# Order of the seven products where a stage ends, and of the last plain part, in a two-layer decoder trunk

## The chip, the cores and the metric

The kernel runs on one core of a Trainium2 chip (trn2). The metric is the device time of one execution in microseconds (us). The engines named below are PE (TensorE, matmuls), DVE (VectorE), ACT (ScalarE), POOL (GpSimd) and SP (SyncE, which here mostly issues loads).

## The reference

The input is 512 tokens of width 1024 in float32. Two layers follow one another, and a last norm closes:

```python
for l in range(DEPTH):                       # DEPTH = 2
    x = x + 0.5 * swiglu(rms_norm(x, ffn1_norm[l]), ffn1_wg[l], ffn1_wu[l], ffn1_wd[l])
    h = rms_norm(x, mix_norm[l])
    z = h @ w_in[l]                          # q, k, v and three conv inputs
    ...                                      # sliding-window attention, short convolution
    x = x + concat([attn_out, conv_out]) @ w_out[l]
    x = x + 0.5 * swiglu(rms_norm(x, ffn2_norm[l]), ffn2_wg[l], ffn2_wu[l], ffn2_wd[l])
return rms_norm(x, final_norm)

def swiglu(h, w_gate, w_up, w_down):         # 1024 -> 2816 -> 1024
    return (silu(h @ w_gate) * (h @ w_up)) @ w_down
```

## The kernel before

**Arithmetic.** Every large product is made of three matmuls: weight and activation are each split in a high and a low part (`wh`, `wl`; `xh`, `xl`), and high x high, high x low and low x high are added in PSUM. The weight split is one copy on ACT and one subtraction on DVE (`split`, L195 and L196). `split_far` (L198) makes the low part in another way: ACT writes the negative, ACT copies, and POOL issues a DMA that adds the raw data.

**Sevens.** Most of the weights are multiplied by a scheme of seven products instead of eight (Strassen-Winograd). Weight quarters and their sums are named a11, a12, s2, s3, s1, a22, s4; the activation quarters and sums that go with them b11, b21, t2, t3, t1, t4, b22. Within b11, b21, b12, b22 the second digit is the half of the tokens (half 0 is tokens 0 to 255). A product of a `share` seven (down projection, or `w_out` in the mixing stage) is two groups of 12 matmuls of 512 columns, 24 matmuls in all. `share` (L751) runs seven steps in the order `CHAINS2`. Each step names an accumulator and an operand. Accumulators x (tag "mm"), y ("sc") and w ("aux") are two PSUM banks each; a step whose flag is False goes on in the banks that hold earlier products. After each step two `scalar_tensor_tensor` on DVE (L771) add the banks to a part of the residual stream `x`: `SHARES` says which column half o, which token half t, and the sign.

```python
CHAINS = (
    ("x", "b11", True), ("w", "b21", True), ("x", "t2", False), ("y", "t3", True),
    ("x", "t1", False), ("y", "t4", False), ("x", "b22", False),
)
CHAINS2 = CHAINS[:4] + (CHAINS[5], CHAINS[4], CHAINS[6])
```

So in a `share` seven y t4 follows y t3, and x t1 is followed by x b22. `Seven.make` prepares the operands: sums on DVE (L540 to L545), then a split on ACT and DVE, or `split_far` for the names in `far` (in the mixing stage t1, t4 and b22).

**Weights.** `order` is the list of weight groups, made by `plan`, and `take_split` takes them one by one. It prepares splits `SPLIT_AHEAD` = 2 groups ahead (`need_split`); `wh` and `wl` have three buffers each. Raw tiles are loaded `LOAD_AHEAD` = 4 units ahead. Sums of weights are made in `need_split`: s2 on DVE (L222, which adds s1 to a11 in place, in the raw tile that a far split's DMA also reads), s4 with an accumulating DMA that POOL issues (`share`) or on DVE (L247). In each feed-forward part that begins with a seven, the first weight group (b = 0, a11, h = 0) is marked "far" and split by `split_far`.

**Stages.** A feed-forward part is a list of stages: "w" sevens for gate and up, "u" a last such block, "p" plain blocks, "s" the down projection of four blocks as a `share` seven, "d" the down projection of single blocks as plain products (`down`, L283, matmuls at L294, additions to x at L1006: for each column half o, for each block, for each of the four token tiles t, 6 matmuls). `FIRST` is the first part of layer 0 and ends with ("s", 6). `INNER` and `LAST` end with ("d", (8, 9, 10)). A mixing stage ends with its `share` seven for `w_out`. In all there are seven `share` sevens that do not end a stage list, and three that do; two of the plain parts of three blocks hand over to a further norm.

**Norm at a stage end.** Where a stage ends, `Norm` is called with `after(t, o)` behind the last addition to each of the eight parts of x. `__call__` squares the part on ACT (L472). When the four parts of a token half are there, `stage` takes the root (an ACT function of another table, so there is a table load before L491), refines it on DVE (L492, L383 to L385), writes xn (L507, DVE), transposes it on PE (L512), and copies the transposes: to a high and low part for a mixing stage (L515 ACT, L516 DVE), or to `hf` for a feed-forward part (L518, ACT), where b11, b21 and t2 are then made at once. `ENDS` says after which step of `share` which part of x is complete. In the last of these norms, `Finale` takes over.

**Order on the engines.** A scheduler orders the instructions of each engine from the program text and the dependences; what the text makes later can be pulled ahead where its operands are there. `tc.issue_after` holds an instruction behind another.

Of the kernel before, what the change touches and what calls it, by code (L numbers as in the profile page):

```python
# [15 lines left out]
P = 128  # L16
D = 1024
S = 512
# [23 lines left out]
SHARED = ("a11", "a12", "s2", "s3", "a22", "s1", "s4")  # L42

SHARES = ((0, 0, 1), (0, 0, 1), (1, 0, -1), (1, 1, 1), (1, 0, 1), (1, 1, -1), (0, 1, 1))
ENDS = {1: (0, 0), 4: (1, 0), 5: (1, 1), 6: (0, 1)}
# [14 lines left out]
CHAINS2 = CHAINS[:4] + (CHAINS[5], CHAINS[4], CHAINS[6])  # L60
# [3 lines left out]
def trunk_kernel(  # L64
# [139 lines left out]
    def need_split(g):  # L204
        while state["split"] <= min(g, len(order) - 1):
# [37 lines left out]
            if isinstance(order[n][1], tuple):  # L243
                if what == "s3" and how == "share":
                    nc.gpsimd.dma_start(out=a12, in_=a11, accum_op=ALU.add)
                elif what == "s3":
                    nc.vector.tensor_add(a12, a12, a11)  # L247
                done = {"s3": (0, 3), "s1": (1,), "a22": (4,), "s4": (2,)}.get(what, ())
                for i in done:
                    del raw_of[u + 2 * i + h]  # L250
# [32 lines left out]
    def down(acts, blocks):  # L283

        for o in range(2):
            accs = [psum("mm", [P, S], f"down_{state['group']}_{t}") for t in range(NT)]
            for i, b in enumerate(blocks):
                _, wh, wl = take_split()
                ah, al = acts[b]
                for t in range(NT):  # L290
                    tok = slice(t * P, (t + 1) * P)
                    for k in range(2):
                        for n, (a, w) in enumerate(((ah, wh), (al, wh), (ah, wl))):
                            nc.tensor.matmul(  # L294
                                accs[t],
                                a[:, k, tok],
                                w[:, k, :],
                                start=i + k + n == 0,
                                stop=i + 1 == len(blocks) and k == 1 and n == 2,
                            )  # L300
                    if i + 1 == len(blocks):
                        yield t, o, accs[t]

    def plan():
# [14 lines left out]

        def seven(at, how, forms=SHARED):  # L320

# [5 lines left out]
            order.extend((u, (what, h, how(what, h))) for what in forms for h in range(2))  # L327

        def ffn(wg, wu, wd, stages):
            for what, b in stages:  # L330
# [4 lines left out]
                if what == "w":  # L335
                    seven(
                        lambda o, j, h: ((wg, wu)[o], KC // 2 * j + 2 * h, 2, 2 * b * P, S),
                        lambda what, h: "far" if (b, what, h) == (0, "a11", 0) else None,
                        FORMS,
# [1042 lines left out]
```

## Time and profile before

| what | value |
|---|---|
| time, median of 3 runs | 1748.76 us |
| lowest, highest | 1743.51, 1749.88 us |
| profiled execution, own time | 1748.8 us |
| its span | 1747.0 us |
| mean granted clock of TensorE | 0.988 |
| busy: PE, DVE, ACT, POOL | 1691.9, 1334.4, 966.9, 194.6 us |
| matmuls | 8150 |

The span is the time from the first to the last recorded instruction of the profiled execution; its own time also holds what lies around it. Places in the profile are given in us from the span's start. The stage ends of interest lie at about 346 (first seven of that kind, into mixing), 517 (mixing into a feed-forward part), 868 (plain part into a feed-forward part), 1219 (plain part into mixing) and 1393 (mixing into a feed-forward part). In rows of single instructions the columns are: start, duration, engine, line, operation, output <- input, shapes, count of neighbours put together, and in brackets the engine's idle time before it with what ended it.

### The profile page before, as it was taken

To read this page: it belongs to the slowest core of one execution; us is meant where nothing else is said; L and a number is where in the kernel's file an instruction comes from. 1 tells how busy PE (TensorE), PEld (TensorE's weight loads), DVE (VectorE), ACT (ScalarE), POOL (GpSimd) and SP (SyncE) were. 2 spreads that over 40 slices of the span, in tenths; PEclk is the share of its full clock that TensorE was granted. 3 is DMA by queue.
4 is the path that set the end of the run, shared out by engine and by line. 5 is a ranking of instruction groups with operands and counts; after the bars stand their busy time and mean duration, and the time that the engine had idled before them with its cause. 6 is when DMAs were issued, how large, how long until landed. Compare 5 with 4: busy or idle time off the path is not lost. (4 is left out here: it accounts for less than half of the span.)

```text
span 1747.0 us, 21808 instructions
## 1 busy us (share of the span) xinstructions
PE 1691.9 (97%) x8150; PEld 1408.2 (81%) x8150; DVE 1334.4 (76%) x1741; ACT 966.9 (55%) x1379; POOL 194.6 (11%) x175
## 2 busy tenths in 40 slices
PE   9999999999989999999999999999999899999998
PEld 7888897798868888877778888877988678888777
DVE  7986689858778776798487776984587797767983
ACT  6545565556666555654365555543465665556553
POOL 0011111000210111110101111100002201111101
PEclk9999999999998999999989999999999999999999
DMA  8467787622695776777637776784126957777771
GB/s 241 108 181 190 184 204 204 158 61 62 163 234 143 186 178 180 192 186 201 145 114 200 182 180 183 193 203 120 37 61 154 242 146 187 176 180 193 189 185 49
DMA packets 188638, 287.19 MB, mean 164 GB/s; under 512 B 9172, under 2 KB 72180, under 8 KB 188532
## 3 DMA queue, kind: packets, MB, share of 16 engines
q1 hardware_dynamic: 146340, 204.91, 36.8%
q0 software_dynamic: 41488, 80.23, 27.2%
q8 instruction: 64, 1.05, 0.2%
q10 hardware_dynamic: 704, 0.66, 0.1%
q14 instruction: 42, 0.34, 0.1%
HBM read 268.46 MB, written 2.10 MB: 155 GB/s over the span
## 5 line engine op out<-in xcount | busy, mean ns | idle before, releaser
L195 ACT CAST wh<-raw 128x1024 fp32r<-128x1024 f32 (+1 forms) x500 | 520.8, 1045 | 572.4 <-PE x L742 134.2
L196 DVE TENSOR_TENSOR wl<-raw,wh 128x1024 fp32r<-128x1024 f32 (+1 forms) x500 | 604.5, 1213 | 291.8 <-ACT wh L195 290.3
L742 PE MATMUL x<-wh,fb 128*128 128x512 f32 x608 | 188.7, 391 | 0.0
L742 PE MATMUL x<-wh,ft 128*128 128x512 f32 x608 | 188.6, 391 | 0.0
L742 PE MATMUL y<-wh,ft 128*128 128x512 f32 x608 | 188.2, 391 | 0.0
L742 PEld LDWEIGHTS x<-wh,fb 128*128 128x128 f32 x608 | 114.4, 188 | 23.5
L742 PEld LDWEIGHTS x<-wh,ft 128*128 128x128 f32 x608 | 113.1, 188 | 22.8
L742 PEld LDWEIGHTS y<-wh,ft 128*128 128x128 f32 x608 | 113.1, 188 | 22.7
L742 PE MATMUL x<-wl,fb 128*128 128x512 f32 x304 | 118.5, 390 | 0.0
L742 PE MATMUL x<-wl,ft 128*128 128x512 f32 x304 | 118.3, 389 | 0.0
L742 PE MATMUL y<-wl,ft 128*128 128x512 f32 x304 | 118.0, 389 | 0.0
L190 POOL DMA_DIRECT2D raw<-in_ffn_wu_dram x42 | 51.1, 1217 | 596.2 <-DVE wl L196 295.2
L742 PE MATMUL w<-wh,fb 128*128 128x512 f32 x304 | 100.6, 415 | 13.3 <-ACT wh L195 10.8
L274 PE MATMUL acc<-hh,wh 128*128 128x512 f32 x240 | 94.6, 394 | 0.0
L277 PE MATMUL acc<-hh,wl 128*128 128x512 f32 x240 | 94.0, 391 | 0.0
L275 PE MATMUL acc<-hl,wh 128*128 128x512 f32 x240 | 93.6, 390 | 0.0
L294 PE MATMUL down<-wh,a 128*128 128x512 f32 x288 | 89.0, 390 | 0.0
L742 PE MATMUL x_s<-wh,ft_s 128*128 128x512 f32 x256 | 79.5, 398 | 8.3 <-ACT wh L195 8.0
L742 PE MATMUL y_s<-wh,ft_s 128*128 128x512 f32 x256 | 80.8, 395 | 3.9 <-ACT wh L195 2.7
L742 PE MATMUL x_s<-wh,fb_s 128*128 128x512 f32 x256 | 80.1, 393 | 3.9 <-DVE x L771 3.6
L222 DVE TENSOR_TENSOR raw<-raw,raw 128x1024 f32<-128x1024 f32 x58 | 70.2, 1219 | 15.7 <-DMA wl<-raw 15.2
L742 PEld LDWEIGHTS w<-wh,fb 128*128 128x128 f32 x304 | 58.5, 198 | 28.0 <-ACT wh L195 13.1
(304 smaller groups left out, 3429.5 us busy)
## 6 DMA issues: line engine op xcount, KB each, us to landing
raw<-in_ffn_wu_dram SPq DMA_DIRECT2D x129, 512.0 KB, 3.7
raw<-in_ffn_wd_dram SPq DMA_DIRECT2D x104, 512.0 KB, 5.1
raw<-in_ffn_wg_dram SPq DMA_DIRECT2D x86, 512.0 KB, 4.8
raw<-in_ffn_wu_dram POOLq DMA_DIRECT2D x42, 512.0 KB, 7.6
raw<-in_ffn_wg_dram POOLq DMA_DIRECT2D x42, 512.0 KB, 7.0
raw<-in_w_in_dram SPq DMA_DIRECT2D x36, 512.0 KB, 3.7
raw<-in_ffn_wd_dram POOLq DMA_DIRECT2D x32, 512.0 KB, 7.3
raw<-raw POOLq DMA_DIRECT2D x20, 512.0 KB, 6.2
```

Of the source, the lines that this page charges most:

```text
L190: nc.gpsimd.dma_start(out=r, in_=rows_of(*more), accum_op=ALU.add)
L195: nc.scalar.copy(hi, raw)
L196: eng.tensor_sub(lo, raw, f32(hi))
L222: nc.vector.tensor_add(a11, a11, s1)
L274: nc.tensor.matmul(acc, hi[:, k, :], rhs[k][0], start=k == first, stop=False)
L275: nc.tensor.matmul(acc, hi[:, k, :], rhs[k][1], start=False, stop=False)
L277: nc.tensor.matmul(acc, lo[:, k, :], rhs[k][0], start=False, stop=k == last)
L294: nc.tensor.matmul(accs[t], a[:, k, tok], w[:, k, :], start=i + k + n == 0, stop=i + 1 == len(blocks) and k == 1 and n == 2,)
L742: nc.tensor.matmul(accs[u], x_[:, 2 * h + k, tok], w[:, k, :], start=start and h + k + i == 0, stop=h + k == 2 and i == 2, skip_group_chec ...
```

## The change

1. `share` sevens that do not end a stage use `CHAINS` itself: y t3, x t1, y t4, x b22, and the weights follow in `FORMS` (s1 ahead of a22).
2. `share` sevens that end a stage ("early": the last of `FIRST` and the two of the mixing stages) use `CHAINS_EARLY`: y t3 ahead of x t2, then y t4, x t1, and the last product in an accumulator z of its own (two "mm" banks). Because z no longer holds x, the sum of x goes to that part as well, in two more DVE additions after x t1. The weights follow in `EARLY`, and POOL's accumulating DMA for s4 moves to s2.
3. The first weight group of a feed-forward part is split plainly, no longer "far".
4. `down` of three blocks: in the second column half all three splits are held, token tiles 0 and 1 run through all blocks first, then tiles 2 and 3 block by block; the next splits are asked for only after each block of this second part.
5. After the first square of a norm one dummy root is computed on ACT.
6. The transposes' copies to `hf` for the second column half go to DVE.

```diff
 FORMS = ("a11", "a12", "s2", "s3", "s1", "a22", "s4")
-SHARED = ("a11", "a12", "s2", "s3", "a22", "s1", "s4")
-
-SHARES = ((0, 0, 1), (0, 0, 1), (1, 0, -1), (1, 1, 1), (1, 0, 1), (1, 1, -1), (0, 1, 1))
-ENDS = {1: (0, 0), 4: (1, 0), 5: (1, 1), 6: (0, 1)}
+EARLY = ("a11", "a12", "s3", "s2", "a22", "s1", "s4")
 SCORES_AT = (5, 6, 7, 8, 9, 10, 12, 13)
...
 )
-CHAINS2 = CHAINS[:4] + (CHAINS[5], CHAINS[4], CHAINS[6])
+SHARES = (
+    ((0, 0, 1),), ((0, 0, 1),), ((1, 0, -1),), ((1, 1, 1),), ((1, 1, -1),), ((1, 0, 1),),
+    ((0, 1, 1),),
+)
+CHAINS_EARLY = (
+    ("x", "b11", True), ("w", "b21", True), ("y", "t3", True), ("x", "t2", False),
+    ("y", "t4", False), ("x", "t1", False), ("z", "b22", True),
+)
+SHARES_EARLY = (
+    ((0, 0, 1),), ((0, 0, 1),), ((1, 1, 1),), ((1, 0, -1),), ((1, 0, 1),),
+    ((1, 1, -1), (0, 1, 1)), ((0, 1, 1),),
+)
+ENDS_EARLY = ((1, (0, 0)), (4, (1, 0)), (5, (1, 1)), (6, (0, 1)))
...
             if isinstance(order[n][1], tuple):
-                if what == "s3" and how == "share":
-                    nc.gpsimd.dma_start(out=a12, in_=a11, accum_op=ALU.add)
-                elif what == "s3":
-                    nc.vector.tensor_add(a12, a12, a11)
-                done = {"s3": (0, 3), "s1": (1,), "a22": (4,), "s4": (2,)}.get(what, ())
+                early = how == "early"
+                if what == "s2" if early else what == "s3":
+                    if how:
+                        nc.gpsimd.dma_start(out=a12, in_=a11, accum_op=ALU.add)
+                    else:
+                        nc.vector.tensor_add(a12, a12, a11)
+                done = {
+                    "s2": (0,) if early else (),
+                    "s3": (3,) if early else (0, 3),
+                    "s1": (1,),
+                    "a22": (4,),
+                    "s4": (2,),
+                }.get(what, ())
                 for i in done:
...
+        last = len(blocks) - 1
+
+        def products(acc, t, i, wh, wl):
+            tok = slice(t * P, (t + 1) * P)
+            ah, al = acts[blocks[i]]
+            for k in range(2):
+                for n, (a, w) in enumerate(((ah, wh), (al, wh), (ah, wl))):
+                    nc.tensor.matmul(
+                        acc,
+                        a[:, k, tok],
+                        w[:, k, :],
+                        start=i + k + n == 0,
+                        stop=i == last and k == 1 and n == 2,
+                    )
+
         for o in range(2):
             accs = [psum("mm", [P, S], f"down_{state['group']}_{t}") for t in range(NT)]
-            for i, b in enumerate(blocks):
+            if o and last:
+                held = [take_split(SPLIT_AHEAD - i)[1:] for i in range(last + 1)]
+                ahead = state["group"]
+                for t in range(2):
+                    for i, w in enumerate(held):
+                        products(accs[t], t, i, *w)
+                    yield t, o, accs[t]
+                for i, w in enumerate(held):
+                    for t in range(2, NT):
+                        products(accs[t], t, i, *w)
+                        if i == last:
+                            yield t, o, accs[t]
+                    need_split(ahead + i)
+                continue
+            for i in range(last + 1):
                 _, wh, wl = take_split()
-                ah, al = acts[b]
                 for t in range(NT):
-                    tok = slice(t * P, (t + 1) * P)
-                    for k in range(2):
-                        for n, (a, w) in enumerate(((ah, wh), (al, wh), (ah, wl))):
-                            nc.tensor.matmul(
-                                accs[t],
-                                a[:, k, tok],
-                                w[:, k, :],
-                                start=i + k + n == 0,
-                                stop=i + 1 == len(blocks) and k == 1 and n == 2,
-                            )
-                    if i + 1 == len(blocks):
+                    products(accs[t], t, i, wh, wl)
+                    if i == last:
                         yield t, o, accs[t]
...
-        def seven(at, how, forms=SHARED):
+        def seven(at, how):
...
                     add_unit(*(at(o, j, h) for o, j in what))
-            order.extend((u, (what, h, how(what, h))) for what in forms for h in range(2))
+            forms = EARLY if how == "early" else FORMS
+            order.extend((u, (what, h, how)) for what in forms for h in range(2))
...
                     seven(
-                        lambda o, j, h: ((wg, wu)[o], KC // 2 * j + 2 * h, 2, 2 * b * P, S),
-                        lambda what, h: "far" if (b, what, h) == (0, "a11", 0) else None,
-                        FORMS,
+                        lambda o, j, h: ((wg, wu)[o], KC // 2 * j + 2 * h, 2, 2 * b * P, S), None
                     )
...
                         lambda o, j, h: (wd, 2 * b + KC // 2 * j + 2 * h, 2, o * S, S),
-                        lambda what, h: "share",
+                        "early" if (what, b) == stages[-1] else "share",
                     )
...
             seven(
-                lambda o, j, h: (w_out[l], KC // 2 * j + 2 * h, 2, o * S, S),
-                lambda what, h: "share",
+                lambda o, j, h: (w_out[l], KC // 2 * j + 2 * h, 2, o * S, S), "early"
             )
...
             )
+            if not any(self.seen):
+                at = o * NT + t
+                nc.scalar.activation(
+                    small(f"table_{self.i}", 1), self.ss[:, at : at + 1], AF.Abs_reciprocal_sqrt
+                )
             half = t // 2
...
             else:
-                nc.scalar.copy(self.full[o][:, :, tok], tp)
+                (nc.vector.tensor_copy if o else nc.scalar.copy)(self.full[o][:, :, tok], tp)
...
         def __init__(self, full, room, name, far=()):
-            self.full, self.room, self.name, self.forms = full, room, name, {}
+            self.full, self.room, self.name, self.forms, self.sums = full, room, name, {}, None
             self.far = far
...
                 )
+                if what in ("t2", "t3") and not self.sums:
+                    self.sums = self.room(self.name)
+                    nc.vector.tensor_sub(self.sums[0], b12, b22)
                 if what == "t2":
-                    self.sums = self.room(self.name)
-                    t3, t2 = self.sums
-                    nc.vector.tensor_sub(t3, b12, b22)
-                    nc.vector.tensor_sub(t2, t3, b11)
+                    nc.vector.tensor_sub(self.sums[1], self.sums[0], b11)
                 if what == "t1":
...
         accs = {}
-        for step, (acc, operand, start) in enumerate(CHAINS2):
+        chains, shares = (CHAINS_EARLY, SHARES_EARLY) if after else (CHAINS, SHARES)
+        for step, (acc, operand, start) in enumerate(chains):
             ops.make(operand)
...
             if start:
-                tag = {"x": "mm", "y": "sc", "w": "aux"}[acc]
+                tag = {"x": "mm", "y": "sc", "w": "aux", "z": "mm"}[acc]
                 accs[acc] = [psum(tag, [P, S], f"{acc}_{ops.name}_{m}") for m in range(2)]
-            o, t, sign = SHARES[step]
             for h in range(2):
...
                     continue
-                for m in range(2):
-                    part = xt(2 * t + m, o)
-                    nc.vector.scalar_tensor_tensor(
-                        part, accs[acc][m], by * sign, part, op0=ALU.mult, op1=ALU.add
-                    )
-                    if after and step in ENDS:
-                        after(2 * t + m, o)
+                for o, t, sign in shares[step]:
+                    for m in range(2):
+                        part = xt(2 * t + m, o)
+                        nc.vector.scalar_tensor_tensor(
+                            part, accs[acc][m], by * sign, part, op0=ALU.mult, op1=ALU.add
+                        )
+                        if after and (step, (o, t)) in ENDS_EARLY:
+                            after(2 * t + m, o)
             if not soon and step < 3:
-                ops.make(CHAINS2[step + 4][1])
+                ops.make(chains[step + 4][1])
             if between:
...
                 then = shared(sevens[1])
-                share(ops, 0.5, ahead(then, {3: ("b11",), 4: ("b21",), 5: ("t2",), 6: ("t3",)}))
+                sums = ("t3", "t2") if stages[-1] == ("s", sevens[1]) else ("t2", "t3")
+                share(
+                    ops, 0.5, ahead(then, {3: ("b11",), 4: ("b21",), 5: sums[:1], 6: sums[1:]})
+                )
             elif what == "s":
...
         after.begin()
-        share(ops, 1.0, soon={(0, 1): ("t2",), (1, 0): ("t1",), (1, 1): ("t3", "t4")}, after=after)
+        share(ops, 1.0, soon={(0, 1): ("t3",), (1, 0): ("t2",), (1, 1): ("t1", "t4")}, after=after)
         state["late"] = None
```

## The prediction

> **What bounds the kernel now.** I read the page first, then TensorE's list of waits, then the windows around the stage changes, then single rows there. The page:
>
> ```profile
> span 1747.0 us, 21808 instructions
> ...
> PE 1691.9 (97%) x8150; PEld 1408.2 (81%) x8150; DVE 1334.4 (76%) x1741; ACT 966.9 (55%) x1379; POOL 194.6 (11%) x175
> ...
> L222 DVE TENSOR_TENSOR raw<-raw,raw 128x1024 f32<-128x1024 f32 x58 | 70.2, 1219 | 15.7 <-DMA wl<-raw 15.2
> ```
>
> TensorE is busy for 97% of the span, and the changed program issues the same number of matmuls, so a gain can only come out of 1747.0 - 1691.9 = 55 us of gaps, out of matmuls slowed by a low clock, and out of short stalls that busy time hides. The profiled execution took 1748.8 us, 1.8 beyond its span, and equals the median of the three runs (1748.76), so I sum against 1748.8. What ends TensorE's gaps (total, times, longest):
>
> ```profile
> PE w L742 <- ACT wh L195: 10.8, 4, 5.6
> PE x_s L742 <- ACT wh L195: 8.0, 6, 2.6
> PE xt L512 <- DVE xn L507: 7.5, 3, 3.9
> ...
> PE x_s L742 <- DVE x L771: 3.6, 6, 0.8
> PE y_s L742 <- ACT wh L195: 2.7, 3, 0.9
> PE w L742 <- ACT fb L195: 2.1, 1, 2.1
> PE x_s L742 <- DVE wl L196: 1.6, 3, 0.5
> ```
>
> Two families: x_s and y_s are the feed-forward sevens, 15.9 us in small waits; w and xt are the first products and the transposes behind a stage end, 20.4 us in a few long ones. In the windows (length, then busy time by engine, then granted clock) the long ones, and one seven, also cost clock:
>
> ```profile
> 522.00:533.00 11.00, 9.19 (x29) 6.78 (x28) 9.31 (x15) 3.24 (x6) 0.00 (x0) 0.53 0.02 3
> 766.00:784.00 18.00, 15.41 (x62) 12.31 (x61) 15.06 (x17) 8.61 (x10) 2.42 (x2) 0.91 0.77 220
> 868.00:888.00 20.00, 13.56 (x54) 10.89 (x54) 15.37 (x28) 11.52 (x23) 0.00 (x0) 0.66 0.07 12
> 1216.00:1236.00 20.00, 16.71 (x112) 15.30 (x111) 15.42 (x31) 10.29 (x20) 0.00 (x0) 0.91 0.18 54
> 1392.00:1412.00 20.00, 14.00 (x56) 10.65 (x57) 17.70 (x23) 8.41 (x15) 0.60 (x1) 0.83 0.31 55
> ```
>
> A clock of 0.66 over 20 us is 13.6 us at half speed; with TensorE busy for two thirds of it, half of that is work not done: 4.6 us. Likewise 4.3 in the first row, 1.4 in the second, 1.5 in the fourth, 2.4 in the fifth.
>
> **Sevens inside a stage (seven of them).** At the first seven of layer 0's second feed-forward:
>
> ```profile
> 772.46 0.39 PE L742 MATMUL y_s<-wl,ft_s 128*128 128x512 f32 x1
> 775.44 2.07 PE L742 MATMUL x_s<-wh,ft_s 128*128 128x512 f32 x4 [2.59 <-ACT wh L195]
> ...
> 788.73 0.70 PE L742 MATMUL x_s<-wh,fb_s 128*128 128x512 f32 x2 [0.61 <-DVE x L771]
> ```
>
> Before, y t3 and y t4 follow each other in the same two banks, so t4 waits for the additions that read t3; the scheduler pulls four matmuls of x t1 ahead of it, and these wait for a split that is made later still. Then x t1 and x b22 meet in the same way (788.73). The change puts x t1 between t3 and t4 and t4 ahead of b22, so the additions of each product lie under the 24 matmuls of the next; the weight sums are re-ordered alike, and a22, whose raw tile comes late, is asked for two groups later. Gone: the x_s rows, 8.0 + 3.6 + 1.6 us, and the 1.4 of clock, 14.6 together. The y_s row (2.7) stays: y t3 begins as before. In the second seven of a stage it may grow by 0.4, three times. **I take 14.** Bounds: 8 (the additions and the wl waits turn up elsewhere: 8.0 + 1.4 - 1.2) and 17 (y_s goes too).
>
> **The two plain parts (d of three blocks), at 868 and 1219.** The second, with a mixing stage behind it:
>
> ```profile
> 1217.72 0.61 PE L294 MATMUL down<-wh,a 128*128 128x512 f32 x2
> ...
> 1218.40 0.61 PE L294 MATMUL down<-wh,a 128*128 128x512 f32 x2
> 1218.85 0.39 PE L294 MATMUL down<-wl,a 128*128 128x512 f32 x1
> 1222.53 2.82 PE L512 MATMUL xt<-ident,xn 128*128 128x128 f32 x12 [3.29 <-DVE xn L507]
> ```
> ```profile
> 1219.28 0.69 DVE L1006 SCALAR_TENSOR_TENSOR x<-down,x 128x512 f32<-128x512 f32 x1 [0.60 <-PE down L294]
> ...
> 1221.73 2.08 DVE L507 SCALAR_TENSOR_TENSOR xn<-x,y,gain 128x512 f32<-128x512 f32 x3
> ...
> 1227.35 1.22 DVE L196 TENSOR_TENSOR wl<-raw,wh 128x1024 fp32r<-128x1024 f32 x1
> ...
> 1232.38 2.47 DVE L516 TENSOR_TENSOR hl<-xt,hh 128x512 fp32r<-128x512 f32 x4
> ```
> ```profile
> 1218.70 0.63 ACT L472 ACTIVATE sq<-x 128x512 bf16<-128x512 f32 x1 [0.61 <-DVE v L490]
> ...
> 1219.44 1.28 ACT L491 ACT_TABLE_LOAD   x1
> 1220.74 0.30 ACT L491 ACTIVATE r<-v,eps 128x2 f32<-128x2 f32 x1
> ```
>
> Three matmuls start in 0.68 us, so one takes 0.227. Half 0's last product ends 12 matmuls (2.7 us) before the end at 1219.24; its transposes start at 1222.53, 6.0 us behind it. With the table load (1.28) moved under the first squares the chain is 4.7, and the change lets half 0 finish 36 matmuls = 8.2 us before the end. So the gap of 3.29 goes, with its 1.5 of clock: 4.8. Half 1 still ends with the last matmul and is next; **I take 4.4**, bounds 2 and 4.8.
>
> At the other one:
>
> ```profile
> 872.13 3.67 PE L512 MATMUL xt<-ident,xn 128*128 128x128 f32 x16 [3.91 <-DVE xn L507]
> 877.95 1.22 PE L742 MATMUL w<-wh,fb 128*128 128x512 f32 x2 [2.15 <-ACT fb L195]
> 879.55 0.80 PE L742 MATMUL w<-wh,fb 128*128 128x512 f32 x1 [0.39 <-DVE fb L196]
> ```
>
> 6.45 us of gaps and 4.6 of clock, 11.1. Here a seven follows, and once the products are out of the way DVE is: for half 1 it has additions 2 x 0.69, xn 4 x 0.69, copies of the transposes 2 x 0.62 (moved to it; priced by the hl row, the same size out of the same memory), the sums and splits of t2 and t3 (4 x 1.22) and three weight splits (3 x 1.22): 13.9 us, against 48 matmuls of half 0 x 0.227 = 10.9. The 3 us short, and some 2.5 of start, remain with their clock: **I take 5.5**, bounds 1 and 11.
>
> **The sevens that end a stage, at 346, 517 and 1393.** The third sum runs ahead of the second, so x t1 carries one more addition each (2 x 0.64) after z, whose 24 matmuls now lie over half 1's chain; z has banks of its own, so nothing waits there. The far split of the next stage's first weight goes:
>
> ```profile
> 517.67 1.22 DVE L222 TENSOR_TENSOR raw<-raw,raw 128x1024 f32<-128x1024 f32 x1 [1.69 <-DMA wl<-raw]
> ...
> 1393.34 1.22 DVE L222 TENSOR_TENSOR raw<-raw,raw 128x1024 f32<-128x1024 f32 x1 [3.29 <-DMA wl<-raw]
> ```
> ```profile
> 519.59 0.63 ACT L472 ACTIVATE sq<-x 128x512 bf16<-128x512 f32 x1 [1.39 <-DVE x L771]
> ...
> 521.30 1.19 PE L742 MATMUL w<-wh,fb 128*128 128x512 f32 x4 [3.71 <-ACT wh L195]
> ...
> 1397.25 2.07 PE L742 MATMUL w<-wh,fb 128*128 128x512 f32 x4 [5.57 <-ACT wh L195]
> ```
>
> DVE's sum at L222 waited for that DMA, behind it an addition, behind that ACT's square, behind that the cast of wh that TensorE waited for. Off the queue: the waits of 1.69 at 517 and 3.29 at 1393, and the sum itself (1.22) at both. On it: two additions, 1.28, and a plain split, 1.22. At 1393 that is 3.29 + 1.22 - 1.28 - 1.22 = 2.0. At 517 the queue alone comes to 0.4; but half 0's chain sheds its table load too (1.28), and the plain split, which now waits for nothing, can be made under x t1, so 0.4 to 2.9. **I take 2 and 2** (bounds: 0, and gap plus clock, 8.0 at both), and **1** at 346, where the gaps are small (bounds 0 and 1.5).
>
> One thing is not removed: t4's split by DMA in the mixing sevens.
>
> ```profile
> 488.53 0.88 POOL L202 DMA_DIRECT2D ft_m<-sums_m  x1 [1.55 <-ACT ft_m L200]
> ...
> 497.45 0.70 PE L742 MATMUL y_m<-wh,ft_m 128*128 128x512 f32 x2 [2.55 <-DVE x L771]
> ...
> DMA to landing us min/median/max: 8.1/8.5/8.9
> ```
>
> TensorE resumed 8.9 us after that issue, so the DMA, not the addition named, was late. The change makes t3 first, t2 next and t4 behind t1, so ACT starts t4's negation about 1.9 us later, while t4 is still third from the end, after x t2: **minus 0.5 at this place and minus 2 at its twin**, bounds 0 and minus 3 each.
>
> Sum: 14 + 4.4 + 5.5 + 2 + 2 + 1 - 2.5 = 26.4 us, so 1748.8 - 26.4 = **1722.4 us**. By lower bounds it is 8 + 2 + 1 - 6 = 5, by upper ones 17 + 4.8 + 11 + 16 + 1.5 = 50.
>
> The table load took 1.28 us in the row, and r started at its end (1219.44 + 1.28, against 1220.74). [...]
>
> **Rivals.** *Only the sevens gain (1735):* the handoffs are DVE's; they give back what they won, as the window at 1392 (DVE 17.7 of 20) allows and the one at 1216 (15.4 busy, gap ended by a chain) speaks against. 1748.8 - 14 = 1735.
>
> *The clock stays full at the stage ends (1713):* a gap of 3.29 and one of 2.59 were followed by half speed, and the change cuts gaps at 521, 872 and 1222. If the remaining ones fall short of what triggers it, 4.3 and 4.6 more come in: 1722.4 - 9 = 1713. [...]
>
> *No change that shows (1745):* the re-ordered sevens wait for their weights at other places (a22 has the latest load), so that of 14 only 4 remain, and handoffs give back theirs. The rows for y_s show that such waits exist, 0.9 each.
>
> *Slower (1758):* DVE becomes the bound at 517, 868 and 1393. New on its queue are two additions, a split and four copies (1.28 + 1.22 + 2.48 = 5.0) at the first and third, 3.7 at the second: 13.7 us, if all of it lands ahead of what TensorE waits for and removing L222 frees nothing. With t4's waits at their bound (6) and a half-speed stretch of 1.7 at two of them, 3.4: 23.1 lost, 14 gained: 1758. It decides where the handoffs lose over 14 + 8.7. For it: DVE is busy 9.31 of 11 us at 522. Against: L222's wait is an idle DVE, and the early half's work moves ahead of the rush.
>
> **How the numbers follow.** About 0.5%, 8.7 us, is what a measurement of this kernel can tell from no change: faster is below 1740. Forecast 0.52 (own range 1715 to 1731), clock full 0.10, only the sevens 0.19, no change 0.11, slower 0.08. Faster is 0.52 + 0.10 + 0.19 = 0.81, same 0.11, slower 0.08. Leaving out the last two cases (0.19), the range runs from 1708, below the full clock's 1713 by the sevens' upper bound, to 1742.
>
> **What would show it.** In the changed profile: x_s waits on wh and x under 3 us together; no gap over 1.5 us ahead of the transposes at the plain parts; no L222 idle on a DMA; clock in the windows at 868 and 1216 nearer to 1; t4's gap still there, 2 to 4 us. Wrong if DVE is busy throughout the handoffs and the w rows grow, or if x_s waits on a load.

## The result, and the profile after

The changed kernel takes 1725.27 us (median of 4 runs, 1724.11 to 1727.49) against 1746.95 us of the kernel before in the same session; the ratio is 0.9878, 95% interval 0.9854 to 0.9902. The forecast was 1722.4, summed against a kernel before of 1748.8.

The top of the page, changed kernel:

```profile
span 1725.7 us, 21836 instructions
...
PE 1685.2 (98%) x8150; PEld 1405.2 (81%) x8150; DVE 1345.7 (78%) x1762; ACT 959.5 (56%) x1369; POOL 191.8 (11%) x172
```

Of the 21.3 us of span that went, 14.6 were gaps of TensorE (1747.0 - 1691.9 = 55.1 before, 1725.7 - 1685.2 = 40.5 after) and 6.7 were busy time of the same 8150 matmuls, so less half speed and fewer stalled starts. By the records of the granted clock, half speed held for 41.0 us before and 27.3 after, the last matmuls of the kernel left aside. TensorE's waits, changed kernel (total, times, longest):

```profile
PE y_m L781 <- DMA ft_m<-sums_m: 9.5, 2, 4.9
PE w L781 <- DVE wl L205: 7.2, 4, 2.7
PE y_s L781 <- ACT wh L204: 5.4, 6, 0.9
PE w L781 <- ACT wh L204: 5.3, 6, 0.9
...
PE xt L551 <- DVE xn L546: 1.1, 6, 0.2
PE x_s L781 <- ACT wh L204: 1.0, 4, 0.3
```

The x_s rows fell from 13.2 us to 1.0 and the transposes' (xt) from 7.5 to 1.1. Two rows took their place at the mixing stages: y_m on t4's DMA, 9.5, and w on a weight's low part (wl) from DVE, 7.2.

Both programs issue 8150 matmuls and the same number up to each stage end, so subtracting the start of the n-th matmul of one trace from that of the other, at the borders of the places, gives what each place saved. All columns but the last two are us saved against the profiled run of before; the last two are the gaps and the busy time of the kernel of the row. The rows below "changed" are the kernels of the experiments:

| kernel | seven inner sevens | end 346 | mixing end 517 | plain 868 | plain 1219 | mixing end 1393 | whole | gaps | PE busy |
|---|---|---|---|---|---|---|---|---|---|
| forecast | 14 | 1 | 2 - 0.5 | 5.5 | 4.4 | 2 - 2 | 26.4 | | |
| changed | 17.1 | 1.7 | -1.3 | 4.2 | 4.6 | -4.9 | 21.4 | 40.5 | 1685.2 |
| inner sevens alone | 16.9 | 0.0 | 2.2 | 0.7 | 0.0 | -4.5 | 14.8 | 45.0 | 1687.2 |
| inner sevens old | 0.6 | 1.6 | -0.4 | 4.3 | 4.7 | -4.1 | 6.3 | 51.3 | 1689.5 |
| ending sevens old | 17.1 | -2.0 | 0.7 | 5.5 | 4.6 | -0.8 | 24.4 | 40.5 | 1682.2 |
| far first split again | 17.1 | 1.6 | 3.7 | 6.3 | 4.7 | -1.6 | 31.9 | 37.0 | 1678.1 |
| old plain part | 17.1 | 1.7 | -1.3 | 1.3 | 1.0 | -5.5 | 13.6 | 46.3 | 1686.9 |
| late table load | 17.2 | 1.0 | -2.4 | 2.7 | 5.3 | -5.7 | 18.1 | 42.4 | 1686.7 |
| copies on ACT | 17.1 | 1.6 | 3.9 | 7.0 | 4.7 | -0.4 | 34.0 | 35.7 | 1677.5 |
| t4 ahead of t1 | 17.0 | 1.6 | 1.4 | 4.6 | 4.6 | -3.0 | 25.7 | 36.9 | 1684.4 |
| t4 plain | 17.2 | 1.6 | 4.6 | 5.3 | 4.8 | 3.1 | 36.7 | 31.9 | 1678.6 |
| t4 plain, copies on ACT | 17.2 | 1.6 | 8.3 | 5.8 | 4.8 | 5.0 | 42.5 | 27.7 | 1677.0 |
| and far first split | 17.2 | 1.7 | 4.1 | 3.9 | 4.7 | 1.0 | 31.8 | 34.4 | 1680.9 |
| or POOL's split | 17.2 | 1.7 | 1.5 | 2.9 | 4.8 | -1.8 | 25.5 | 40.5 | 1681.1 |

Places that a kernel does not touch agree to 0.2 at the sevens and at 1219, but move by about 1 us at 868, and at the two mixing ends, which the inner sevens alone do not touch either, by 2.2 and 4.5. There lie the gaps of which some were followed by half speed and some were not (2.55 us was, 3.39 was not; last section).

**Sevens.** The first seven of layer 0's second feed-forward in the changed kernel:

```profile
760.43 0.73 PE L781 MATMUL y_s<-wh,ft_s 128*128 128x512 f32 x2 [0.90 <-ACT wh L204]
...
770.54 1.07 PE L781 MATMUL x_s<-wh,ft_s 128*128 128x512 f32 x4
...
781.42 0.62 PE L781 MATMUL x_s<-wh,fb_s 128*128 128x512 f32 x2
```

x t1 (770.54) and x b22 (781.42) start without a gap; before, 2.59 and 0.61 stood there. The 0.90 ahead of y t3 stays.

**Plain part into mixing:**

```profile
1198.00 0.66 PE L551 MATMUL xt<-ident,xn 128*128 128x128 f32 x4 [0.17 <-DVE xn L546]
...
1204.40 0.39 PE L309 MATMUL down<-wl,a 128*128 128x512 f32 x1
1204.62 0.28 PE L1192 MATMUL acc<-hh,wh 128*128 128x256 f32 x1
...
1209.30 0.63 PE L551 MATMUL xt<-ident,xn 128*128 128x128 f32 x4 [0.20 <-DVE xn L546]
```

Half 0's transposes now stand among the last products, 6.8 us ahead of their end, and the next stage's product follows the last one at once.

**Mixing end at 517.** The DMA for t4, TensorE's wait for it, and DVE's queue behind the seven:

```profile
486.92 0.88 POOL L211 DMA_DIRECT2D ft_m<-sums_m  x1 [1.22 <-ACT ft_m L209]
...
496.47 1.22 PE L781 MATMUL y_m<-wh,ft_m 128*128 128x512 f32 x2 [4.62 <-DMA ft_m<-sums_m]
...
522.46 0.79 PE L781 MATMUL w<-wl,fb 128*128 128x512 f32 x1 [2.74 <-DVE wl L205]
```
```profile
512.98 1.28 DVE L557 COPY hf<-xt 128x512 f32<-128x512 f32 x2
...
516.52 1.28 DVE L811 SCALAR_TENSOR_TENSOR x<-x_m,x 128x512 f32<-128x512 f32 x2
517.72 2.35 DVE L205 TENSOR_TENSOR wl<-raw,wh 128x1024 fp32r<-128x1024 f32 x2
519.99 1.28 DVE L811 SCALAR_TENSOR_TENSOR x<-z_m,x 128x512 f32<-128x512 f32 x2
521.19 1.22 DVE L205 TENSOR_TENSOR wl<-raw,wh 128x1024 fp32r<-128x1024 f32 x1
```

TensorE wanted t4 at 496.47 - 4.62 = 491.85, 4.9 us behind the issue; before it wanted it 494.90 - 488.53 = 6.4 behind. At 522 it waits for the last of a row of DVE operations without a pause: copies, additions, low parts.

Windows of the changed kernel (as before: length, busy by engine, clock):

```profile
484.00:500.00 16.00, 10.49 (x38) 7.89 (x37) 9.72 (x11) 8.50 (x13) 2.95 (x3) 0.84 1.02 294
516.00:536.00 20.00, 15.40 (x66) 11.49 (x65) 19.11 (x27) 8.17 (x15) 1.20 (x1) 0.91 0.25 42
845.00:875.00 30.00, 26.33 (x120) 20.13 (x119) 22.88 (x36) 12.73 (x22) 1.37 (x2) 0.94 0.27 53
1180.00:1215.00 35.00, 34.63 (x200) 29.82 (x198) 23.08 (x39) 17.41 (x33) 0.00 (x0) 1.00 0.28 81
```

At the plain part into mixing the clock is 1.00 over 35 us (before 0.91 over 20 us), at the other one 0.94 over 30 us (before 0.66 over 20 us). Behind the mixing stage DVE is busy 19.1 of 20 us, ACT 8.2.

### The profile page after: what moved, and what is told of

Its sections match the earlier page's. It is cut to its first block, busy times and chain, and to the rows that moved or that the text cites. A ratio compares the mean times of both kernels' runs of the same rounds, so it can differ in the third digit from the quotient of the medians.

```text
span 1725.7 us, 21836 instructions
## 1 busy us (share of the span) xinstructions
PE 1685.2 (98%) x8150; PEld 1405.2 (81%) x8150; DVE 1345.7 (78%) x1762; ACT 959.5 (56%) x1369; POOL 191.8 (11%) x172
## 4 chain that ended last, share of the span: by engine, by line
PE 59%; DVE 6%; issue 2%; ACT 1%; DMA 1%; POOL 0%; ACTq 0%; POOLq 0%; DVEq 0%
PE x L781 18%; PE y L781 9%; PE x_s L781 6%; PE w L781 4%; PE y_s L781 4%; PE down L309 3%; PE x L896 2%; PE acc L291 2%; PE acc L292 2%; PE acc L294 2%; PE at L982 2%; DVE wl L205 1%; PE y L896 1%; DVE raw L231 1%; PE acc L1192 1%
## 5 line engine op out<-in xcount | busy, mean ns | idle before, releaser
L199 POOL DMA_DIRECT2D raw<-in_ffn_wg_dram x42 | 50.9, 1219 | 244.6 <-DVE wl L205 92.3
L781 PE MATMUL x_s<-wh,fb_s 128*128 128x512 f32 x240 | 74.0, 389 | 0.0
```

What stands on the lines that cost most here:

```text
L199: nc.gpsimd.dma_start(out=r, in_=rows_of(*more), accum_op=ALU.add)
L781: nc.tensor.matmul(accs[u], x_[:, 2 * h + k, tok], w[:, k, :], start=start and h + k + i == 0, stop=h + k == 2 and i == 2, skip_group_chec ...
```

## The experiments

Each was compared with the kernel before on its own chip; medians of before there were 1752.18 (first four kernels), 1747.49 (next four) and 1750.74 (last four). The changed kernel was not run beside them, and before moves by 5 us from one of these to the next, so differences from the changed kernel are read from the traces, one of each kernel.

**The inner sevens alone,** on the kernel before:

```diff
-        for step, (acc, operand, start) in enumerate(CHAINS2):
+        chains, shares = (CHAINS2, SHARES) if after else (CHAINS, SHARES_IN)
+        for step, (acc, operand, start) in enumerate(chains):
...
+            if forms is SHARED and not last:
+                forms = FORMS
```

> The kernel before with part 1 of the change alone: the seven sevens that do not end a stage run y t3, x t1, y t4, x b22 with their weights in that order; the three that end a stage, the plain parts, the norm and the first split stay as they were. Theory: these sevens carry most of the gain by themselves. Between the stage ends the two traces differ by 1.9 us in the first feed-forward part, 6.6, 3.7 and 4.8 us in the next three, 17.0 together, so 17 us less than the kernel before (1730 against 1747), and no x_s row over 1.5 us in the list of waits. Rival: the sevens only hand their gain to the stage end behind them, which waits for DVE anyway; then less than 9 us.

Measured: 1732.31 us, ratio 0.9886 (0.9856 to 0.9916). As the theory had it: by place the sevens give 16.9 of the 17.1, and the stage ends do not take it back, except 4.5 at 1393, where nothing of the seven was edited. Three queues show why, ACT, DVE, then PE:

```profile
1357.79 1.99 ACT L196 CAST wh<-raw 128x1024 fp32r<-128x1024 f32 x2 [4.23 <-DMA raw<-in_w_out_dram]
```
```profile
1358.87 1.23 DVE L197 TENSOR_TENSOR wl<-raw,wh 128x1024 fp32r<-128x1024 f32 x1 [4.05 <-ACT wh L196]
1360.01 1.28 DVE L776 SCALAR_TENSOR_TENSOR x<-y_m,x 128x512 f32<-128x512 f32 x2
```
```profile
1360.85 0.76 PE L746 MATMUL y_m<-wh,ft_m 128*128 128x512 f32 x2 [4.66 <-DVE x L776]
```

In the old order y t4 has a second wait: the addition that frees y's banks stands behind a weight split whose load is late. Here that wait was the later one; why the load came late in this kernel is not shown.

**The inner sevens old,** in the changed kernel:

```diff
-        chains, shares = (CHAINS_EARLY, SHARES_EARLY) if after else (CHAINS, SHARES)
+        chains, shares = (CHAINS_EARLY, SHARES_EARLY) if after else (CHAINS2, SHARES2)
...
+            forms = EARLY if how == "early" else SHARED if how else FORMS
```

> The changed kernel with part 1 taken back. Theory, if the parts add up: 17 us above the changed kernel, 1742, which is 5 us below the kernel before, the sum of what the stage ends gave. Rival (the parts overlap, the stage ends need the sevens' new order): within 5 us of the kernel before or above it, 1745 to 1750.

Measured: 1744.02 us, ratio 0.9968 (0.9949 to 0.9987). The time alone, 2 to 9 us below the kernel before, does not exclude the rival; the places do. The parts add up: 14.8 with the sevens alone and 6.3 without them make 21.1 of 21.4.

**t4 ahead of t1:**

```diff
-        share(ops, 1.0, soon={(0, 1): ("t3",), (1, 0): ("t2",), (1, 1): ("t1", "t4")}, after=after)
+        share(ops, 1.0, soon={(0, 1): ("t3",), (1, 0): ("t2",), (1, 1): ("t4", "t1")}, after=after)
```

> The changed kernel, but in the two mixing stages t4 is prepared ahead of t1, as its product now also comes ahead of t1's. Theory: the 4.62 and 4.91 us gaps in the mixing sevens are t4's split by DMA, issued too late. ACT's negative and copy of t1 (2.0 us) no longer stand in front, so the gaps shrink by 2.0 us each, to 2.6 and 2.9; half speed stays, since 2.55 was followed by it: 4 us less than the changed kernel, 1721. If 2.6 falls under what lowers the clock, 7 us less. Rival: the gap belongs to the additions in DVE's queue, as the row of before named them; then no change (1725), the gaps ended by DVE.

**t4 split plainly:**

```diff
-        ops = Seven(mixed, room_g8, f"m_{l}", far=("t1", "t4", "b22"))
+        ops = Seven(mixed, room_g8, f"m_{l}", far=("t1", "b22"))
```

> The changed kernel, but t4 of the two mixing sevens is split by ACT and DVE, without the DMA. Theory: both gaps go (4.62 and 4.91 us) and the half speed behind them (1.7 us each); DVE gets 1.22 us more at each place, which may delay the next weight split by as much (a gap of 0.88 there becomes 2): 13 less 2.4, so about 11 us below the changed kernel, 1714 (1711 to 1718). Rival: DVE is the bound of these stage ends (19.1 of 20 us busy from 516 on), so what is won at t4 is lost behind it: less than 4 us, 1721 or more.

Measured: 1721.71 us, ratio 0.9829 (0.9800 to 0.9858), and 1712.05 us, ratio 0.9775 (0.9752 to 0.9799). With t4 ahead the two gaps are 2.73 and 3.19 (4.62 and 4.91 in the changed kernel), still ended by the DMA, and the span is 4.4 us shorter, as the theory had it. Its half speed was right at one place only: no half speed followed the 2.73, it did follow the 3.19, and behind the seven at 517 there was more of it than in the changed kernel (10.2 us for 3.4), so that the size of 4 came out partly by luck. With t4 plain the span is 15.2 us shorter where the theory had 11; TensorE's row for t4's DMA is gone, and a wl wait beside it grew from 1.7 to 2.3:

```profile
PE w L781 <- DVE wl L205: 7.2, 4, 2.7
PE y_s L781 <- ACT wh L204: 5.4, 6, 0.9
PE w L781 <- ACT wh L204: 5.1, 6, 0.9
PE x_m L781 <- DVE wl L205: 2.3, 2, 1.5
```

So in the changed kernel the gap is the DMA's, and with the clock it is worth 15.2 us of span (1725.7 against 1710.5), 8.6 of it gaps.

**The old plain part:**

```diff
-            if o and last:
+            if o and last > 9:
```

> The changed kernel with part 4 taken back: the plain part of three blocks runs block by block in both column halves. Theory: half 0 ends 12 matmuls (2.7 us) before the last one again. At the one into mixing its chain of 6.0 less the table load's 1.28 leaves a gap of 2.0; at the other one 3.91 less 1.28 is 2.6, which is long enough for half speed: 2 + 2.6 + 2, so 6 to 7 us above the changed kernel, 1732 against 1725.3. Rival: the table load and the copies made these two gains, and the plain part's order little; then less than 2 us.

Measured: 1733.24 us, ratio 0.9913 (0.9882 to 0.9944). The two places lose 3.0 and 3.6, 6.6 together, and the transposes wait again. The total is the theory's, its parts are not. At 1219 the gap is 2.1, as expected, but half speed followed it (3.4 us). At 868 there are two gaps, of 4.50 and 2.19, where one of 2.6 was expected; against that the changed kernel's four waits of 0.7 to 1.0 for w are gone there:

```profile
PE xt L551 <- DVE xn L546: 9.3, 6, 4.5
```

**The far split of the first weight again:**

```diff
+                order.extend(
+                    (u, (what, h, "far" if (what, h) == ("a11", 0) else None))
+                    for what in forms
+                    for h in range(2)
+                )
```

> The changed kernel with part 3 taken back: the first weight group of a feed-forward part that starts with a seven is split by ACT and an adding DMA. Theory: the sum that DVE makes in place of that raw tile waits for the DMA again, with additions and weight splits queued behind it: 2 us each behind the two mixing stages, about 1 behind the plain part, so 1730. Rival: DVE is full there (19.1 of 20 us from 516 on), and 1.22 us less on it counts for more than the wait: 1 us less at each place, 1722.

Measured: 1719.08 us, ratio 0.9832 (0.9796 to 0.9868), against the theory and beyond the rival. DVE's sum does not wait for that DMA any more. The group L231 in the changed kernel, and in this one:

```profile
L231 DVE TENSOR_TENSOR raw<-raw,raw 128x1024 f32<-128x1024 f32 x58 | 70.3, 1220 | 0.5
```
```profile
L231 DVE TENSOR_TENSOR raw<-raw,raw 128x1024 f32<-128x1024 f32 x58 | 70.3, 1220 | 1.0 <-DMA raw<-in_ffn_wu_dram 0.5
```

In the kernel before this row had 15.7, nearly all for the DMA. Here DVE has so much ahead of the sum that the DMA has landed when it gets there; the plain split's 1.22 is only one more item in the row. Without it TensorE's wait for wl falls from 2.74 to 1.60 at both mixing ends.

**The table load in its old place:**

```diff
-            if not any(self.seen):
+            if False:
```

> The changed kernel with part 5 taken back: no dummy root, so the table load of 1.28 us stands in half 0's chain before the root. Theory: behind the plain parts it costs nothing (chain 6.0 against 8.2 us of products that lie over it); behind the three sevens that end a stage half 0's transposes come 1.28 us later into a row of products that PE takes in order: up to 1.28 at each, so 2 us above the changed kernel, 1727 (1725 to 1729). Rival: the chain of half 0 sets the stage ends; then 1.28 at all five, 6.4 us: 1732.

Measured: 1730.92 us, ratio 0.9900 (0.9870 to 0.9931). The span grew by 3.4 us: 0.7 at 346, and 1.1, 1.6 and 0.8 at the three ends with a seven behind them; at 1219 nothing was lost. That is more than the theory's 2 and less than the rival's 6.4; the 1.6 at the plain part at 868, where the theory had nothing, makes most of the difference. DVE's low part for w then comes later still (9.1 us in TensorE's list, 7.2 in the changed kernel's).

**The copies on ACT:**

```diff
-                (nc.vector.tensor_copy if o else nc.scalar.copy)(self.full[o][:, :, tok], tp)
+                nc.scalar.copy(self.full[o][:, :, tok], tp)
```

> The changed kernel with part 6 taken back: all copies of the transposes are ACT's. Theory (DVE is the bound behind the mixing stages and behind the plain part into a feed-forward part): four copies of 0.68 us leave DVE at three places, and ACT, 8 of 20 us busy there, has room: 1 to 2 us less at each, 1721. Rival: ACT takes its copies one after the other, so that b21 is ready later than with two engines copying; 1 us more at each, 1728.

Measured: 1717.10 us, ratio 0.9822 (0.9789 to 0.9854): the theory, and more. Its gaps are 4.8 us smaller than the changed kernel's (35.7 against 40.5). Of these 2.4 are the relief of DVE at the two mixing ends (the waits for wl of 2.74 become 1.55 and 1.51), but 1.9 lie at t4, ahead of the copies: its DMA landed 8.5 and 9.0 us behind its issue, against 9.5 and 9.7 in the changed kernel. The other 7.7 us of the 12.5 of span are busy time, for the most part clock (half speed for 6.8 us in all, 27.3 in the changed kernel). Two windows and TensorE's wait between them show how:

```profile
484.00:500.00 16.00, 11.50 (x49) 8.85 (x48) 10.79 (x13) 9.75 (x14) 3.49 (x4) 1.00 1.02 285
500.00:506.00 6.00, 5.82 (x28) 4.52 (x26) 5.17 (x12) 3.64 (x7) 1.10 (x1) 1.00 0.88 179
```
```profile
495.55 0.74 PE L781 MATMUL y_m<-wh,ft_m 128*128 128x512 f32 x2 [3.39 <-DMA ft_m<-sums_m]
```

The gap for t4 was 3.39 here, and no half speed followed it. The kernel with the far split has the same (3.49, clock 1.00). So the gains of these two overstate their edits: of 4.8 and 3.5 us of gaps, 1.9 and 1.7 are t4's DMA landing sooner, which nothing here ties to the edit, and much of the clock went with where a gap fell (last section).

**The ending sevens in their old order:**

```diff
-    ("x", "b11", True), ("w", "b21", True), ("y", "t3", True), ("x", "t2", False),
-    ("y", "t4", False), ("x", "t1", False), ("z", "b22", True),
+    ("x", "b11", True), ("w", "b21", True), ("x", "t2", False), ("y", "t3", True),
+    ("y", "t4", False), ("x", "t1", False), ("x", "b22", False),
```

> The changed kernel with part 2 taken back: the three sevens that end a stage run in their old order (x t2, y t3, y t4, x t1, b22 in x's banks), with t3 and t4 prepared as before. Theory: t4's DMA is again issued as early against its use as before (gaps of 2.55 and 1.94 instead of 4.62 and 4.91), which takes off 7.5 us by the places in the two traces (3.0 and 4.5); the new order's own worth, z over half 1's chain, is lost: 1 at the first such seven and 2 to 3 at each mixing stage. Net 1 to 2 us below the changed kernel, 1723. Rival: the new order is worth nothing behind the mixing stages; then 6 us below, 1719. Second rival: it is worth more than t4 costs; then above 1728.

Measured: 1721.10 us, ratio 0.9835 (0.9804 to 0.9865); the span is 3.0 us below the changed kernel's, between theory and rival. At 346 the new order is worth 3.7 us within the changed kernel, more than I gave it; 2.0 of it is a loss against the kernel before, which the other parts bring there (TensorE waits 1.9 for an addition) and the new order removes. At the mixing ends it costs 2.0 and 4.1 (t4's gaps are 3.22 and 1.82 without it, 4.62 and 4.91 with it): it moves t4 closer to its DMA and gains there less than that. Its old waits come back in their place:

```profile
PE x_m L780 <- DVE x L810: 5.7, 2, 2.9
...
PE y_m L780 <- DMA ft_m<-sums_m: 5.0, 2, 3.2
```

**t4 plain and copies on ACT; with the far split; with POOL's split.** The first is the two edits above together. The second adds the edit of the far split. The third gives the low part of the first two weight groups to POOL:

```diff
-                split(hi, lo, raw)
+                eng = nc.gpsimd if isinstance(what, str) and isinstance(order[n][1], tuple) and how == "pool" else nc.vector
+                split(hi, lo, raw, eng)
```

> The changed kernel with t4 split plainly and the copies of the transposes back on ACT. Theory: the two gains lie at different places (t4 ahead of the stage end, the copies behind it) and add up: 13.2 us for t4, and by place 1.7, 1.7 and 2.8 us for the copies, 6.2: 19.4 less than the changed kernel, 1706. Rival: without the gap at t4 DVE comes to the stage end later, and the copies' gain is used up: 1711.

> The kernel with t4 plain and copies on ACT, and also the first weight group split by the adding DMA again (part 3 taken back). Theory: DVE is still the bound behind the stages, so 1.22 us less on it counts once more: 1 us at each of three places, 3 less than without it, 1703. Rival: with DVE relieved it reaches the sum earlier and waits for the DMA, as in the kernel before: 0 to 3 us more than without it, 1708.

> The kernel with t4 plain and copies on ACT, and the low part of the first two weight groups made by POOL's own subtraction (by its rows of 1.29 us for half the size an estimated 2.6 each) instead of DVE's. Theory: DVE loses 2.4 us of work at three places and waits for no DMA: 1.5 us less at each, 1702. Rival: POOL is slow and its loads stand behind it, so that the sum of weights waits for it: 1706 or more.

Measured: 1706.89 us, ratio 0.9750 (0.9720 to 0.9779); 1716.20 us, ratio 0.9802 (0.9767 to 0.9838); 1721.16 us, ratio 0.9833 (0.9803 to 0.9862). The first came out as its theory had it and is the fastest kernel of the case. In gaps its two edits add up: 8.6 for t4 plain and 4.2 more for the copies, of which 2.4 are waits for wl at the mixing ends. In busy time they do not (PE 1678.6 and 1677.5 alone, 1677.0 together): half speed held for 17.1, 6.8 and 10.2 us.

The far split, with 3.5 us of gaps less in the changed kernel, costs 6.7 us of gaps here. L231 with it:

```profile
L231 DVE TENSOR_TENSOR raw<-raw,raw 128x1024 f32<-128x1024 f32 x58 | 70.3, 1221 | 7.8 <-DMA wl<-raw 4.4 <-ACT wh L204 2.9
```

With DVE relieved, its queue reaches the sum before the DMA has landed, and the wait of the kernel before is in part back. POOL's split does the same in another way, on POOL and DVE:

```profile
509.44 2.85 POOL L205 TENSOR_TENSOR wl<-raw,wh 128x1024 fp32r<-128x1024 f32 x1
...
512.54 3.29 POOL L205 TENSOR_TENSOR wl<-raw,wh 128x1024 fp32r<-128x1024 f32 x1
```
```profile
512.32 4.60 DVE L231 TENSOR_TENSOR raw<-raw,raw 128x1024 f32<-128x1024 f32 x1 [2.83 <-POOL wl L205]
```

The sum waits 2.83 us for POOL's reading of the raw tile, and then takes 4.60 us instead of 1.22, beside POOL's second split.

## Why the prediction was right, and where it was not

The sign, the size and the shape held: 21.4 us of span came where 26.4 were forecast, and the measured median lies 2.9 us above the forecast, inside the forecast's own range. That it lies so near is partly luck: the kernel before measured 1.8 us less than the 1748.8 that the sum began from, and the sevens, with 3 us more than forecast, made up for part of t4, with 5 us less. By its steps:

- **Inner sevens, 14: 17.1.** The mechanism is shown by the kernel that has this part alone and the one without it. The term was too small because it was made of listed gaps: in the seven sevens the listed gaps shrank by 11.2 us, and a half-speed stretch worth 1.6 went. The 15 stalls that went also cost 0.16 each that no gap shows, 2.5 together: matmuls start 0.227 apart, and the one before a stall still counts as busy for its 0.39. Starts that are late without any gap make the last 1.6. The y_s row rose from 2.7 to 5.4, 0.9 at three more places, where 0.4 at each had been allowed for.
- **Plain part into mixing, 4.4: 4.6; into a feed-forward part, 5.5: 4.2.** Right. Taking the plain part's order back loses 3.6 and 3.0; the table load is not needed for it at 1219, as the chain with the load in it, 6.0 against 8.2 us, said. At the other one the copies that went to DVE cost up to 2.8 (7.0 with them on ACT), which the step had put into DVE's row.
- **The first ending seven, 1: 1.7.** The bound of 1.5 from visible gaps was a little low, for the same reason as in the sevens: of the 1.7 only 0.8 are gaps.
- **t4's DMA, minus 2.5: minus 7.5** (3.0 at 488, 4.5 at its twin, by the finer borders there). This is the term that was mis-sized most. The direction was right, and the kernel with t4 plain shows it. The step had the issue 1.9 us later and the use in its old place, which by itself is 1.9 here, and yet put 0.5 into the sum. The issue did come 1.8 later, counted by matmuls; TensorE wanted t4 4.9 us behind the issue, not 6.4, and TensorE resumed 9.6 us behind the issue (486.92 to 496.47), not 8.9. Behind each gap there was also one more half-speed step of 3.4 us, up to 1.7 lost, which the step did not count. I also said of the kernel before that the DMA, not the addition named, was late. That was not shown: 488.53 + 8.9 = 497.43 and the addition's end fall together, and the kernel with the inner sevens alone has the addition as the later one.
- **Mixing ends, 2 and 2: 1.8 and -0.4** behind t4. The 2 at 517 is right by luck: the gaps there did not shrink (5.5 and 5.4 us), and the gain is half speed, 10.2 us before and 3.4 after. At 1393 the gaps shrank by 1.6, near the step's 2.0, and half speed grew from 6.8 to 10.2 us. For both ends the step counted the two additions and the split, but left out the four copies on DVE, 2.5 us, that it had itself listed under the rival "slower". With the copies on ACT this stretch gains 3.5 at both places.
- **The far split.** The step took its removal as a gain. The opposite is shown for the changed kernel: with it back, TensorE's waits for wl at the mixing ends are 1.1 us shorter each. The removal is a gain only where DVE comes early to the sum; that is shown for the kernel with t4 plain and copies on ACT. For the kernel before only the wait of 15.7 speaks for it, no run.
- **What was to show it.** x_s waits 1.0 us (under 3), the transposes' gaps at the plain parts are 0.2 (under 1.5), L231 idles 0.5 us where L222 had 15.7, the clock at 868 and 1219 rose; t4's gap is 4.6 to 4.9, above the 2 to 4 named. Of the sign for "wrong", half came true: DVE is busy throughout the ends, but the w rows fell, from 14.4 to 12.5 us.
- **Rivals.** "Only the sevens gain" has a part of truth: the two mixing ends gave back 6.1 us. DVE as the bound of the stage ends (19.1 of 20 us) is there, but it did not outweigh.

## What to carry to other kernels

When an order is changed, an operand whose preparation moves back must still be ready for its use: compare issue to use, not issue to issue, for each operand that comes by DMA. Moving an operation off an engine helps only while that engine is what the next stage waits for; here the far split shortened TensorE's waits for wl at the mixing ends by 1.1 us each where DVE was full, and cost 6.7 us of gaps where it was relieved, so such choices are tried again after each change. Gains read from one trace hold what the clock did in it; the waits at the place of the edit say what the edit did. A list of gaps understated what a stall between dependent products cost, here by 0.16 us a stall.

## What was not expected of the hardware

The length of a gap alone did not tell whether half speed followed. In the kernel before, the gap of 2.55 us at 497 was followed by it:

```profile
500.00:502.00 2.00, 2.00 (x7) 1.52 (x6) 0.00 (x0) 0.64 (x1) 0.46 (x1) 0.50 1.03 360
```

With the copies on ACT 3.39 us at the same place was not, with the far split 3.49 was not, and in the changed kernel 4.62 was (0.84 in the window from 484). The records of the granted clock in the 14 traces say more. In each of them all half-speed stretches begin on one grid of 3.41 us (at 498.81, 522.71 and 775.29 in the kernel before, at 495.02, 522.32 and 870.48 in the changed one) and, but for the last one, last a whole number of its steps. Leaving out the first and last 30 us, half speed followed all 49 steps at full clock in which TensorE was idle for 2.05 us or more (6 of them in the kernel before, 4 in the changed one), none with less than 1.5, and 8 of the 24 between (it followed 1.59 in the changed kernel, not 1.63 there and not 1.71 in the kernel before); what decides those is open. The gap of 2.55 put 2.05 us into one step, the gap of 3.39 was divided into 1.92 and 1.47 (the first number behind each length is TensorE's busy time, the clock is the third from the end):

```profile
495.40:498.81 3.41, 1.35 (x6) 1.17 (x7) 3.33 (x4) 1.00 (x2) 0.00 (x0) 1.00 1.03 356
498.81:502.22 3.41, 3.41 (x10) 2.63 (x9) 0.23 (x1) 0.86 (x1) 0.68 (x1) 0.50 1.02 369
```
```profile
490.66:494.08 3.42, 1.50 (x7) 0.92 (x5) 3.42 (x4) 2.07 (x3) 0.00 (x0) 1.00 1.08 274
494.08:497.49 3.41, 1.94 (x8) 1.61 (x9) 1.22 (x2) 0.00 (x0) 0.00 (x0) 1.00 1.00 358
```

So in these traces half speed went with how much of one step was idle, not with the length of the gap. The grid lies otherwise in each trace (498.81, 495.02 and 490.66 are starts of steps in the kernel before, the changed kernel and the one with the copies on ACT), and what sets its place is not shown. The rival in which the clock stays full turned on the length of the gaps that remain; by these rows the length does not settle it. The time of one kernel moved as well: beside the last eight kernels, the kernel before took from 1743.14 us, at a mean clock of 0.991, to 1757.46, at 0.984. By these clocks alone that is, as an estimate, up to 0.007 x 1750 = 12 us; that the place of the gaps made it is a guess of mine.

POOL's subtraction of 128 x 1024 took 2.85 and 3.29 us, and an addition on DVE beside it 4.60 instead of 1.22.
